# Transposing 128 keys' probabilities where the 16 meta keys are wanted, in the attention of a hybrid streaming encoder

## The chip, the cores and the metric

The kernel runs on one core of a Trainium2 chip. The metric is the device time of one launch in microseconds (us); three runs of a kernel give a median. The core has five engines with a queue of instructions each: TensorE (PE, with its weight loads shown apart as PEld), VectorE (DVE), ScalarE (ACT), GpSimd (POOL) and SyncE (SP), which here issues the DMA transfers.

## The reference, cut to what matters

One layer of a trunk over 2048 frames, with 16 learned "meta" tokens put in front (2064 positions). A combined projection feeds two mixers, an RWKV-7 recurrence and a forgetting attention with 8 heads of width 64; their outputs go through one output projection and a ConvFFN. The change lies in the attention:

```python
q = _rmsnorm(_heads(q, FX_HEADS), q_g).astype(f32) * (HEAD_DIM ** -0.5)
k = _rmsnorm(_heads(k, FX_HEADS), k_g).astype(f32)
c = jnp.cumsum(logf, axis=1)
...
    s = jnp.einsum('bhqd,bhkd->bhqk', q_i, k) + c_i[..., None] - c[:, :, None, :]
    s = jnp.where(kpos[None, :] <= pos_i[:, None], s, -jnp.inf)
    p = jax.nn.softmax(s, axis=-1)
    return jnp.einsum('bhqk,bhkd->bhqd', p, v)
```

## The kernel before, in words

**Attention.** Queries are cut into one block of the 16 meta tokens (called i = -1) and 16 blocks of 128 frames. Keys are cut in the same way: key block 0 holds the 16 meta keys, the others 128 keys each. `softmax` multiplies queries and keys in pieces of up to 512 keys into PSUM tiles `s` (two matmuls, L952 and L954, of which the second adds the low part `kl` of the keys), adds the decay row `cb` and keeps a running minimum on VectorE (L945), and takes the exponential of the whole row on ScalarE (L971) into `P`, 128 queries x all keys seen.

**Values.** `value` takes two query blocks at a time. For every key block it transposes the probabilities on TensorE into a PSUM tile `pt` (L1002: the piece of `P` is the stationary operand, an identity matrix the moving one), makes a high and a low part of the result (`ph` by a cast on ScalarE, L1017; `pl` by a subtraction on VectorE, L1018) and multiplies both with the values `vs` into the tile `o` (L1022). Key block 0 is treated apart: its transpose yields 16 rows, which go into rows 0 to 15 (high) and 32 to 47 (low) of a tile `meta` (L1011, L1012), and one matmul (L1013) adds them to `o`. There are 8 heads x 16 blocks = 128 of these 16-key transposes for blocks of 128 queries, and 8 for the block of 16 queries.

**Heads.** `load_head` brings a head's keys and queries in pieces (`raw`, L892), casts them on ScalarE (L893, L896) and subtracts on GpSimd (`kl` L894, `kq` L897); it also loads the decay row, repeated over 128 partitions (`cb`, L885, 1032 KB). `attention` is built twice: "at" (query blocks up to 7, two heads' buffers) and "at2" (query blocks 8 to 15, in which the tiles of a head, `kq`, `kl`, `cb` and `vs`, have one buffer, so that the next head's loads wait for the last score of the head before). The heads of at2 are numbered 1 to 8 below.

**What stands around it.** While the attention runs, matmuls of the projection phase (L203 to L205) and then of the output projection and the FFN (L1096) are mixed in between as filler; their weights come in pieces of 512 KB (`ww_raw`, L78), are split on ScalarE and VectorE (`ww_hi` L81, `ww_lo` L82). `xh` is the normed input of the FFN.

**What sets the order.** Nothing in the source fixes how attention and filler alternate on an engine. The whole program is built with `schedule_with_timeline_sim=True`: when the program is built, a scheduler places every instruction on a simulated timeline, and each engine's queue gets the instructions in that order. Queues run strictly in that order.

Of the kernel before, what the change touches and what calls it, by code (L numbers as in the profile page):

```python
# [855 lines left out]
def attention(K, ctx, name, phases, bufs, banks):  # L856


    nc = K.nc
# [115 lines left out]
    def keys(j):  # L975
        return (0, 16) if j == 0 else (16 + 128 * (j - 1), 128)

    def value(hd, qt, soft):

        vs, qa = hd[4], hd[6]  # L980
        nqs = [16 if i < 0 else 128 for i in qt]
        Ps, inv = zip(*soft)
        q0 = 0 if qt[0] < 0 else 16 + 128 * qt[0]
        N = sum(nqs)
        per = 2 if N <= 256 else 1
        shape = [128, per, 512 // per]
        o = ps([128, 512], "o", no)[:, :N]
        nt = qt[-1] + 2
        j = 0
        while j < nt:  # L990
            js = [j] if j == 0 else list(range(j, min(j + per, nt)))
            pt = ps(shape, "pt", npt)
            kn = keys(j)[1]
            if j:
                ph, pl = sp(shape, "ph", nph, F32R), sp(shape, "pl", nph, F32R)
            cols = []
            for x, jj in enumerate(js):
                k0, kn = keys(jj)
                c0 = 0
                for P, i, nq in zip(Ps, qt, nqs):  # L1000
                    if jj <= i + 1:
                        nc.tensor.transpose(pt[:kn, x, c0 : c0 + nq], P[:nq, k0 : k0 + kn], K.ident[:nq, :nq])  # L1002
                    c0 += nq
                cols.append(sum(nq for i, nq in zip(qt, nqs) if jj > i + 1))
            if len(set(cols)) == 1:
                views = [(slice(0, len(js)), cols[0])]
            else:
                views = [(slice(x, x + 1), c) for x, c in enumerate(cols)]
            if j == 0:
                c, p0 = cols[0], meta  # L1010
                nc.scalar.copy(p0[:kn, c:N], pt[:kn, 0, c:N])  # L1011
                nc.vector.tensor_sub(p0[32 : 32 + kn, c:N], pt[:kn, 0, c:N], p0[:kn, c:N].bitcast(F32))  # L1012
                nc.tensor.matmul(o[:, c:N], vs[:, 0], p0[:, c:N], start=True, stop=False)  # L1013
                j = 1
                continue
            for xs, c in views:
                nc.scalar.copy(ph[:kn, xs, c:N], pt[:kn, xs, c:N])  # L1017
                nc.vector.tensor_sub(pl[:kn, xs, c:N], pt[:kn, xs, c:N], ph[:kn, xs, c:N].bitcast(F32))  # L1018
            for x, jj in enumerate(js):
                c = cols[x]  # L1020
                for y, pp in enumerate((ph, pl)):
                    nc.tensor.matmul(o[:, c:N], vs[:kn, jj], pp[:kn, x, c:N], start=False, stop=jj == nt - 1 and y == 1)  # L1022
            j += len(js)
        o2 = sp([64, NQ], "o2", min(nhead, 2))[:, :N]
        nc.scalar.copy(o2, o[64:128])
        nc.vector.tensor_tensor(o2, o2, o[0:64], op=ALU.add)

        rp = ps([128, 512], "s", ns)[:, :N]
        c0 = 0
        for r, nq in zip(inv, nqs):  # L1030
            e = sp([128, 128], "E", 2)[:nq]
            nc.gpsimd.tensor_scalar(e, r.to_broadcast([nq, 128]), 1.0, 0.0, op0=ALU.mult, op1=ALU.add)
            nc.tensor.transpose(rp[:, c0 : c0 + nq], e, K.ident[:nq, :nq])
            c0 += nq
        rb = sp([64, NQ], "rb", min(nhead, 2))[:, :N]
        nc.scalar.copy(rb, rp[:64])
        og = hd[5][:, q0 - qa : q0 - qa + N]
        nc.gpsimd.tensor_tensor(og, og, rb, op=ALU.mult)
        nc.vector.tensor_tensor(og, o2, og, op=ALU.mult)

    def finish(hd, h, qt, soft, last):
        value(hd, qt, soft)
        if last:
            p_, hh = divmod(h, 2)
            og, qa = hd[5:]
            nc.sync.dma_start(K.yd[4 + p_, 64 * hh : 64 * hh + 64, qa : qa + og.shape[1]], og)
# [274 lines left out]
```

## Time and profile before

| | |
|---|---|
| median of 3 runs | 3427.64 us (3419.93 to 3429.69) |
| profiled execution | 3421.68 us, its span 3419.8 us |
| PE busy | 3321.0 us, 97% of the span |
| PEld, DVE, ACT, POOL busy | 2941.8, 2301.7, 1653.1, 1165.1 us |
| TensorE clock over the span | 0.987 of full speed |

The profile is of one execution. [...] The attention stands between 1218 and 2340 us of the span.

### The profile page before, as it was taken

The page shows a single profiled execution, that of the slowest core. Times are in us where ns is not written, and L with a number is a line of the kernel's source. Part 1 is how long each engine was busy: PE and PEld are TensorE (multiplying, and loading weights), DVE is VectorE, ACT ScalarE, POOL GpSimd, SP SyncE. Part 2 cuts the span into 40 slices and gives each one's busy share as a digit, 9 for nine tenths or more (in the row PEclk, how much of TensorE's full clock was granted, in tenths as well). Part 3 has the DMA queues.
Part 4 walks back from the last instruction along what each step waited for, and adds up shares of the span by engine and source line. Part 5 has one row for each costly group of instructions (what it writes and reads, how often), then busy time and mean ns, then how long its engine had stood idle before and what let it go on. Part 6 is the DMA issues. An engine that isn't in the chain of part 4 may idle for free.

```text
span 3419.8 us, 62536 instructions
## 1 busy us (share of the span) xinstructions
PE 3321.0 (97%) x23259; PEld 2941.8 (86%) x23259; DVE 2301.7 (67%) x4849; ACT 1653.1 (48%) x3450; POOL 1165.1 (34%) x2055
## 2 busy tenths in 40 slices
PE   7999999999999999999999999999999999999999
PEld 7889888988988988999999998888887888878887
DVE  5655566566556657888878886777665666646666
ACT  5543444554244467765666665654333333333332
POOL 4441113344111167755444454422114211132121
PEclk9999999999999999999999999999999999999999
DMA  4556333355634255333333343223324323232222
GB/s 114 119 123 161 105 95 99 102 124 130 156 88 105 84 173 160 112 103 109 94 93 94 93 137 117 86 82 129 104 89 159 97 90 97 93 116 94 93 93 92
DMA packets 352888, 376.57 MB, mean 110 GB/s; under 512 B 169112, under 2 KB 281992, under 8 KB 351560
## 3 DMA queue, kind: packets, MB, share of 16 engines
q1 hardware_dynamic: 352392, 372.52, 38.2%
q8 instruction: 183, 3.00, 0.4%
q14 instruction: 121, 0.99, 0.1%
q0 software_dynamic: 192, 0.07, 0.0%
HBM read 302.22 MB, written 70.27 MB: 109 GB/s over the span
## 4 chain that ended last, share of the span: by engine, by line
PE 51%; DVE 2%; DMA 2%; POOL 2%; issue 2%; ACT 2%; SPq 0%; POOLq 0%; ACTq 0%; DVEq 0%
PE pp L1096 30%; PE pr L1096 12%; PE o L1022 3%; PE pt L1002 3%; DMA raw<-d_qk 2%; PE s L952 1%; PE s L954 1%; DVE ww_lo L82 1%; POOL xl L1158 0%; POOL kl L894 0%; DVE P L945 0%; DVE pl L1018 0%; ACT P L971 0%; DMA cb<-d_cd 0%; ACT ph L1017 0%
## 5 line engine op out<-in xcount | busy, mean ns | idle before, releaser
L82 DVE TENSOR_TENSOR ww_lo<-ww_raw,ww_hi 128x1024 fp32r<-128x1024 f32 (+1 forms) x304 | 375.4, 1244 | 248.7 <-PE pp L1096 128.9
L81 ACT CAST ww_hi<-ww_raw 128x1024 fp32r<-128x1024 f32 (+1 forms) x304 | 307.6, 1025 | 387.9 <-PE pp L1096 140.0
L1096 PE MATMUL pp<-xh,ww_hi 128*128 128x512 f32 (+2 forms) x1952 | 432.3, 353 | 11.4 <-ACT xh L1157 6.0
L1096 PE MATMUL pp<-xh,ww_lo 128*128 128x512 f32 (+2 forms) x1952 | 429.1, 351 | 0.0
L1096 PE MATMUL pp<-xl,ww_hi 128*128 128x512 f32 (+2 forms) x1952 | 428.4, 350 | 0.3 <-POOL xl L1158 0.3
L1096 PEld LDWEIGHTS pp<-xh,ww_hi 128*128 128x128 f32 x1952 | 324.8, 190 | 66.5 <-ACT xh L1157 11.1
L1096 PEld LDWEIGHTS pp<-xl,ww_hi 128*128 128x128 f32 x1952 | 326.2, 189 | 52.8 <-POOL xl L1158 1.0
L1096 PEld LDWEIGHTS pp<-xh,ww_lo 128*128 128x128 f32 x1952 | 325.3, 189 | 47.4
L1179 POOL TENSOR_SCALAR c<-c,pc 128x1 f32<-128x1 f32 x220 | 84.7, 385 | 611.2 <-ACT c L1176 609.8
L1018 DVE TENSOR_TENSOR pl<-pt,ph 128x512 fp32r<-128x512 f32 (+2 forms) x352 | 196.1, 562 | 51.7 <-ACT ph L1017 50.1
L1191 POOL TENSOR_TENSOR zl<-cv,zh 128x512 fp32r<-128x512 f32 (+1 forms) x110 | 119.8, 1089 | 312.7 <-ACT zh L1190 302.3
L945 DVE CUSTOM_DVE_ANT_0 P<-cb,s 16x16 f32<-16x16 f32 (+8 forms) x360 | 182.7, 519 | 53.6 <-PE s L954 29.1
L1017 ACT CAST ph<-pt 128x512 fp32r<-128x512 f32 (+2 forms) x352 | 167.8, 486 | 103.4 <-PE pt L1002 72.9
L1204 DVE TENSOR_TENSOR acc<-acc,pr 128x512 f32<-128x512 f32 x240 | 164.5, 688 | 73.5 <-PE pr L1096 69.1
L1002 PE MATMUL pt<-cst,P 128*128 128x128 f32 (+2 forms) x1224 | 202.6, 277 | 2.6 <-ACT P L971 1.5
L1173 ACT ACTIVATE cv<-pp,pc 128x510 f32<-128x510 f32 (+1 forms) x220 | 151.9, 691 | 84.3 <-PE pp L1096 82.9
L89 POOL TENSOR_TENSOR wi<-sq,kx 128x320 fp32r<-128x320 f32 (+2 forms) x48 | 48.2, 1003 | 389.9 <-ACT kx L88 290.1
L203 PE MATMUL pj<-xah,w_hi 128*128 128x384 f32 x480 | 165.8, 346 | 1.6 <-ACT xah L194 1.6
L1177 DVE SCALAR_TENSOR_TENSOR cv<-pp,pc,cv 128x511 f32<-128x511 f32 (+1 forms) x220 | 140.7, 639 | 36.0 <-ACT c L1176 35.9
L205 PE MATMUL pj<-xah,w_lo 128*128 128x384 f32 x480 | 164.4, 342 | 0.4 <-DVE w_lo L82 0.4
L204 PE MATMUL pj<-xal,w_hi 128*128 128x384 f32 x480 | 163.6, 341 | 0.0
L1022 PE MATMUL o<-ph,vs 128*128 128x256 f32 x576 | 158.1, 284 | 5.5 <-ACT ph L1017 5.2
(393 smaller groups left out, 8668.8 us busy)
## 6 DMA issues: line engine op xcount, KB each, us to landing
ww_raw<-in_fin_dram SPq DMA_DIRECT2D x176, 512.0 KB, 3.6
ww_raw<-in_fout_dram SPq DMA_DIRECT2D x88, 512.0 KB, 3.7
w_raw<-in_wt_dram SPq DMA_DIRECT2D x60, 512.0 KB, 3.8
xv<-d_var SPq DMA_DIRECT2D x32, 384.0 KB, 6.0
ww_raw<-in_wo_dram SPq DMA_DIRECT2D x24, 512.0 KB, 3.6
raw<-d_qk SPq DMA_DIRECT2D x112, 88.0 KB, 2.7
cb<-d_cd SPq DMA_DIRECT2D x8, 1032.0 KB, 6.6
out_dram<-acc SPq DMA_DIRECT2D x32, 256.0 KB, 2.8
```

The source lines that it names most:

```text
L81: nc.scalar.copy(hi, raw)
L82: nc.vector.tensor_sub(lo, raw, hi.bitcast(F32))
L203: nc.tensor.matmul(p, wh[:, c, :M], xh[:, c, :n], start=c == 0, stop=False)
L204: nc.tensor.matmul(p, wh[:, c, :M], xl[:, c, :n], start=False, stop=False)
L205: nc.tensor.matmul(p, wl[:, c, :M], xh[:, c, :n], start=False, stop=c == KC - 1)
L945: nc.vector.tensor_tensor_reduce(dst, c, src, 1.0, 3e38, op0=ALU.add, op1=ALU.min, accum_out=mx[:nq, np_ : np_ + 1])
L1002: nc.tensor.transpose(pt[:kn, x, c0 : c0 + nq], P[:nq, k0 : k0 + kn], K.ident[:nq, :nq])
L1017: nc.scalar.copy(ph[:kn, xs, c:N], pt[:kn, xs, c:N])
L1018: nc.vector.tensor_sub(pl[:kn, xs, c:N], pt[:kn, xs, c:N], ph[:kn, xs, c:N].bitcast(F32))
L1022: nc.tensor.matmul(o[:, c:N], vs[:kn, jj], pp[:kn, x, c:N], start=False, stop=jj == nt - 1 and y == 1)
L1096: self.K.nc.tensor.matmul(p, w, x, start=i == 0, stop=i == len(mms) - 1)
L1204: nc.vector.tensor_tensor(a, a, p, op=ALU.add)
```

## The change

For blocks of 128 queries the transpose of key block 0 now takes the first 128 columns of `P` (`kt`), the 16 meta keys and the first 112 frame keys, and writes 128 rows of `pt`. The cast and the subtraction behind it still read 16 rows. The block of 16 queries keeps its 16 keys. The 2 lines that are added shift the line numbers behind them: L1002 becomes L1004, L1022 becomes L1024, L1096 becomes L1098.

```diff
                     if jj <= i + 1:
-                        nc.tensor.transpose(pt[:kn, x, c0 : c0 + nq], P[:nq, k0 : k0 + kn], K.ident[:nq, :nq])
+
+                        kt = 128 if i >= 0 else kn
+                        nc.tensor.transpose(pt[:kt, x, c0 : c0 + nq], P[:nq, k0 : k0 + kt], K.ident[:nq, :nq])
                     c0 += nq
```

The instructions are the same ones in number and, but for these 128, in shape. Their order is not: from about 1255 us of the span, some ten of these transposes into the attention, to about 2400 us the scheduler mixes attention and filler in another way on all five queues; before and after that stretch the queues are the same. A row below names the output tile, the inputs and the output's shape; the number at a tile's end tells its uses apart.

**TensorE, the change of head 6 to head 7 of at2** (`kq_22265` is head 7's; `pp` rows are filler). Before:

```order
L1096 MATMUL pp_29316<-xl_29098,ww_hi_29312 128x512 x5
L1096 MATMUL pp_29316<-xh_29097,ww_lo_29313 128x512 x7
L1022 MATMUL o_22151<-ph_22224,vs_21620 128x256
L1096 MATMUL pp_29316<-xh_29097,ww_lo_29313 128x512
L1096 MATMUL pp_29351<-xh_29097,ww_hi_29347 128x512 x4
L1022 MATMUL o_22151<-pl_22225,vs_21620 128x256
L1022 MATMUL o_22151<-ph_22224,vs_21620 128x256
L1022 MATMUL o_22151<-pl_22225,vs_21620 128x256
L1022 MATMUL o_22151<-ph_22237,vs_21620 128x256
L952 MATMUL s_22352<-kq_22265 128x400
```

In the changed kernel, at the same place:

```order
L1004 MATMUL pt_22425<-cst_72,P_22122 128x128
L1015 MATMUL o_22392<-meta_18159,vs_21620 128x256
L1024 MATMUL o_22392<-ph_22400,vs_21620 128x256
L1024 MATMUL o_22392<-pl_22401,vs_21620 128x256
L1024 MATMUL o_22392<-ph_22400,vs_21620 128x256
L1024 MATMUL o_22392<-pl_22401,vs_21620 128x256
L1024 MATMUL o_22392<-ph_22413,vs_21620 128x256
L952 MATMUL s_22352<-kq_22265 128x400
```

The 43 filler matmuls of 512 columns that stood between the last score of head 6 and the first score of head 7 have moved ahead of that last score; in their place stand the first products of the next pair of blocks (`o_22392`), which stood behind it before.

**ScalarE, the change of head 2 to head 3 of at2** (`ph_19417` belongs to head 2's last product, `kq_19445` to head 3's loads). Before:

```order
L1017 CAST ph_19417<-pt_19416 128x256
L893 CAST kq_19445<-raw_19458 128x336
L893 CAST kq_19445<-raw_19463 128x176
L896 CAST kq_19445<-raw_19463 128x176
L1017 CAST ph_19417<-pt_19416 128x128
L1190 CAST zh_26731<-cv_26836 128x258
```

In the changed kernel:

```order
L1019 CAST ph_19417<-pt_19416 128x256
L1019 CAST ph_19417<-pt_19416 128x128
L893 CAST kq_19445<-raw_19458 128x336
L893 CAST kq_19445<-raw_19463 128x176
L896 CAST kq_19445<-raw_19463 128x176
L1013 CAST meta_18159<-pt_19573 16x256
```

The last piece of `ph_19417` has moved from behind the three casts of freshly loaded pieces to ahead of them.

## Rows read from the trace of the kernel before

**Rows 1.** The page's head: span, instructions, busy time and share of each engine.

```profile
span 3419.8 us, 62536 instructions
PE 3321.0 (97%) x23259; PEld 2941.8 (86%) x23259; DVE 2301.7 (67%) x4849; ACT 1653.1 (48%) x3450; POOL 1165.1 (34%) x2055
```

**Rows 2.** Busy time by stretch: window, length, PE, PEld, DVE, ACT, POOL, granted clock, DMA.

```profile
1255.00:2400.00 1145.00, 1114.80 (x7854) 1036.03 (x7853) 901.71 (x2483) 714.25 (x1564) 564.90 (x1123) 0.99 0.37 111
...
1753.25:1756.60 3.35, 3.35 (x17) 3.35 (x16) 2.48 (x6) 1.78 (x5) 1.71 (x3) 0.50 0.41 107
1756.70:1800.00 43.30, 43.30 (x348) 42.78 (x347) 34.64 (x107) 28.95 (x66) 23.66 (x53) 1.00 0.33 94
...
2099.00:2132.00 33.00, 28.72 (x171) 24.21 (x171) 22.31 (x60) 20.49 (x43) 16.19 (x25) 1.00 0.29 82
```

**Rows 3.** Groups of L1002 by shape: busy us, mean ns, idle time before.

```profile
L1002 PE MATMUL pt<-cst,P 128*128 128x128 f32 x1088 | 175.8, 277 | 1.0 <-DVE meta L1012 1.0
L1002 PE MATMUL pt<-cst,P 128*16 128x128 f32 x128 | 30.2, 279 | 0.4 <-ACT P L971 0.2
...
L1002 PEld LDWEIGHTS pt<-cst,P 128*128 128x128 f32 x1088 | 128.1, 142 | 3.6 <-DVE meta L1012 1.6
...
L1002 PEld LDWEIGHTS pt<-cst,P 128*16 128x16 f32 x128 | 10.7, 89 | 1.9 <-ACT P L971 0.9 <-DVE pl L1018 0.2
```

**Rows 4.** Timeline of PE: start, length, line and shape, count of merged matmuls.

```profile
1908.17 0.60 PE L1002 MATMUL pt<-cst,P 128*128 128x128 f32 x4
...
1917.23 0.75 PE L1096 MATMUL pp<-xh,ww_lo 128*128 128x256 f32 x5
1917.81 0.28 PE L1022 MATMUL o<-ph,vs 128*128 128x256 f32 x1
...
1918.40 0.38 PE L1002 MATMUL pt<-cst,P 128*16 128x128 f32 x2
...
2088.06 2.03 PE L1096 MATMUL pp<-xh,ww_lo 128*128 128x512 f32 x8
2089.93 0.39 PE L1096 MATMUL pp<-xh,ww_hi 128*128 128x512 f32 x1
```

**Rows 5.** Scores (L952) at each change of head in at2, heads 2 to 8: first and last start.

```profile
L952 PE MATMUL s<-kq x2: 346/348/350, 1653.7 to 1665.9; 128*128 128x400 f32 x2
L952 PE MATMUL s<-kq x2: 427/554/682, 1738.6 to 1755.8; 128*128 128x400 f32 x2
L952 PE MATMUL s<-kq x2: 341/344/348, 1824.6 to 1836.5; 128*128 128x400 f32 x2
L952 PE MATMUL s<-kq x2: 340/396/451, 1906.9 to 1919.8; 128*128 128x400 f32 x2
L952 PE MATMUL s<-kq x2: 344/345/346, 1994.2 to 2007.8; 128*128 128x400 f32 x2
L952 PE MATMUL s<-kq x2: 341/382/424, 2084.7 to 2098.7; 128*128 128x400 f32 x2
L952 PE MATMUL s<-kq x2: 342/386/430, 2183.9 to 2196.9; 128*128 128x400 f32 x2
```

**Rows 6.** Timelines of POOL at the changes to heads 3, 4, 5 and 7.

```profile
1753.25 0.56 POOL L897 TENSOR_TENSOR kq<-raw,kq 64x176 fp32r<-64x176 f32 x1
...
1835.17 0.56 POOL L897 TENSOR_TENSOR kq<-raw,kq 64x176 fp32r<-64x176 f32 x1
...
1919.24 0.55 POOL L897 TENSOR_TENSOR kq<-raw,kq 64x176 fp32r<-64x176 f32 x1
...
2094.01 0.88 POOL L964 TENSOR_TENSOR cm<-cb,cst 128x128 f32<-128x128 f32 x2 [3.80 <-DMA cb<-d_cd]
...
2098.10 0.56 POOL L897 TENSOR_TENSOR kq<-raw,kq 64x176 fp32r<-64x176 f32 x1
```

**Rows 7.** Timelines of ACT and PE at the change to head 3; idle time before in brackets.

```profile
1750.82 0.80 ACT L893 CAST kq<-raw 128x336 fp32r<-128x336 f32 x2 [5.15 <-DMA raw<-d_qk]
...
1752.08 0.33 PE L1022 MATMUL o<-ph,vs 128*128 128x128 f32 x1 [3.58 <-ACT ph L1017]
```

## The prediction

> **What bounds the kernel now.** The page's head comes first: TensorE is busy for 97% of the span, no other engine for more than 67% [rows 1]. So the time is TensorE's work plus its gaps, and a change can act in two ways: it makes TensorE's work longer or shorter, or it moves gaps. The table of stretches shows the room for the second. The change touches the queues from 1255 to 2400 us; there TensorE is idle for 1145.0 - 1114.8 = 30.2 us [rows 2]. Next, the groups of L1002 by shape and TensorE's timeline price the transposes [rows 3, 4]. Last, the timelines at the places where a head of at2 gives way to the next show what decides whether TensorE waits there [rows 5 to 7]. A difference of 0.3%, 10.3 us, is about what a measurement of this kernel can tell from none.
>
> **The wider transposes.** 128 transposes take 128 columns of P as stationary operand where they took 16. The matmul streams the same 128 columns of the identity: 279 ns in the narrow form and 277 in the wide [rows 3]. What matters is what one costs in a row of them. Four wide ones take 0.60 us, so each after the first adds (0.60 - 0.28) / 3 = 0.11 us; two narrow ones take 0.38 us, so the second adds 0.38 - 0.28 = 0.10 us [rows 3, 4]. Both forms step alike. The weight load does grow, from 89 to 142 ns, 53 ns [rows 3]. It runs beside the matmul before it, and is seen only where the load itself was held back by a wait. All waits ahead of the 128 narrow loads come to 1.9 us [rows 3]. The bounds are 0 (every load hidden) and 128 x 53 ns = 6.8 us (none hidden). I take 0.5 us, some ten exposed loads, near the lower bound, since 1.9 us of waiting is the sum of few waits.
>
> [...]
>
> ScalarE's cast and VectorE's subtraction read 16 rows as before, and the wide form reads only what one exponential wrote for the whole row, so no new wait comes with it.
>
> **The changed order, at the changes of head.** In at2 a head's tiles have one buffer. Between the last score of a head and the first score of the next lies a chain: the last score frees the buffers, casts (L893) and subtractions (L894) of waiting pieces run, further pieces and the 1032 KB of `cb` are loaded, cast, and subtracted, and the first score waits for `kq` (L897). TensorE must fill that time with other rows of its queue. From the last score's start to the end of that `kq` the chain took 1753.81 - 1738.6 = 15.2 us for head 3, 1835.73 - 1824.6 = 11.1 for head 4, 1919.79 - 1906.9 = 12.9 for head 5 and 2098.66 - 2084.7 = 14.0 for head 7 [rows 5, 6]. In the last the wait for `cb` is plain, and the first score follows at 2098.7 [rows 5, 6].
>
> TensorE's work in between I count from the two orders, with a step of (2089.93 - 2088.06) / 8 = 0.233 us for a matmul of 512 columns, (1917.81 - 1917.23) / 5 = 0.12 for 256, and 0.11 for a transpose [rows 4]. For head 7, before: 43 x 0.233 + 17 x 0.11 + 15 x 0.12 + 0.36 for two score matmuls = 14.0 us, as long as the interval itself, no gap. After: 31 transposes, 24 products of 256 columns, two of 128 (0.06 each) and the two score matmuls, 3.4 + 2.9 + 0.1 + 0.4 = 6.8 us, and no filler at all. If the chain stays, TensorE stands for 14.0 - 6.8 = 7.2 us. Counted alike for heads 2 to 8, the work is 12.2, 11.6, 11.9, 11.7, 12.4, 14.0 and 12.9 us before and 13.6, 12.1, 10.0, 10.8, 15.2, 6.8 and 13.6 after. The intervals of before are 12.2, 17.2, 11.9, 12.9, 13.6, 14.0 and 13.0 us [rows 5], so before lost 0 + 5.6 + 0 + 1.2 + 1.2 + 0 + 0.1 = 8.1 us there. After, with the same chains, heads 2, 6 and 8 have more work than their interval and lose nothing; heads 3, 4, 5 and 7 lose 15.2 - 12.1 = 3.1, 11.1 - 10.0 = 1.1, 12.9 - 10.8 = 2.1 and 7.2, in all 13.5. That is **+5.4 us**. With the shortest chain seen, 11.1, everywhere, after would lose 0 + 1.1 + 0.3 + 4.3 = 5.7 us, or -2.4; I take the chains as they were, since the order of loads ahead of `cb` changes little.
>
> The gap of head 3 is not simply won, though the order removes its visible cause. A cast of `ph` stood behind three casts of pieces not yet landed; ScalarE waited 5.15 us for them and TensorE 3.58 us for `ph` [rows 7]. Now the cast stands ahead of them. But the pieces land no earlier, and what is late next is the first score of head 3; hence the 3.1 us above.
>
> **Two smaller terms.** [...] A gap of 7 us at head 7 should bring another: **+1.2**. Against that, the first products of the next pair (`o_22392`) ran from 2099 to 2132 us in a stretch with 33.0 - 28.7 = 4.3 us of idle [rows 2]; they now stand inside the wait: **-4.3**.
>
> **Sum.** 0.5 + 5.4 + 1.2 - 4.3 = +2.8 us on the profiled execution's 3421.7: 3424.5. That execution lies 6.0 us below the median of the runs, 3427.6; on the median the forecast is 3430.4, about 3430. The rest of the idle time, 30.2 - 4.3 - some 5 at the changes of head = 21 us, is dealt out anew by the new order; I see no reason for more or less of it.
>
> **The rivals.** (a) *Slower: the chains at the changes of head grow.* With chains of c us at all of them, after loses (4c - 39.7) at heads 3, 4, 5, 7 and 2(c - 13.6) at heads 2 and 8; with -8.1, +0.5, -4.3 and three more spells of half clock (3.6) that is 6c - 75.2. It passes 10.3 us from c = 14.3 on, and at head 3's 15.2 it is +16.0, 3443.6 us. For it: head 3 and head 7 had 15.2 and 14.0. Against: heads 4 and 5 had 11.1 and 12.9, and less filler in a wait also means fewer weight loads in the DMA queues. Chance 0.22. (b) *Faster: the new order fills gaps.* Of the 21 us elsewhere some 13 would have to go, beside the +2.8, to leave 3417. For it: the gaps are many, and such a one as at head 3 is undone in the order. Against: gaps of the same kind arise anew. Chance 0.11. (c) *The loads are not hidden:* 6.8 for 0.5, or 3436.7 us, still within 0.3%; slower only if waits add to it. Chance 0.04, half of it beyond. (d) *The narrow form has a hidden price*, so that the wide one is faster by itself: 2 ns of mean length x 128 = 0.3 us is all that the rows allow, and 80 ns each would be needed to be seen; chance 0.02. [...]
>
> **Chances and range.** The forecast, within 0.3%, has 0.61 and half of (c) adds 0.02: 0.63. Slower by more: 0.22 + 0.02 = 0.24. Faster by more: 0.11 + 0.02 = 0.13. The range goes from 3420, where half of the idle time elsewhere has gone (-10), to 3442, just short of (a)'s full price; about 0.08 is left out on either side.
>
> **What would show it.** L1004's 128 weight loads at about 142 ns and a step of 0.11 us; the changes of head as intervals between L952 of two heads, with about 14 us at head 7 and a TensorE gap of some 7 us in it, and half clock behind; the 3.58 us wait for `ph` gone and the wait at the first score of head 3; less idle between 2099 and 2132 us. I would be wrong if `kq` of head 7 came within 9 us of the last score, or if large gaps arose where I have not counted.

## The result and the profile after

The changed kernel took 3441.4 us, the median of 7 executions (3437.4 to 3446.7), the kernel before 3427.5 beside it. The ratio is 1.0051, with a 95% interval of 1.0033 to 1.0069: slower, by 14 us where +2.8 were forecast. In a later comparison the same program measured 1.0076 (after_again, below).

The page's head of the changed kernel, which answers to [rows 1]:

```profile
span 3440.9 us, 62529 instructions
PE 3324.6 (97%) x23259; PEld 2948.4 (86%) x23259; DVE 2314.6 (67%) x4849; ACT 1655.8 (48%) x3450; POOL 1167.4 (34%) x2055
```

The span grew by 21.1 us and TensorE's busy time by 3.6: TensorE has as much work as before and waits longer. Busy time by stretch (columns as in [rows 2]) tells where:

```profile
1255.00:2400.00 1145.00, 1099.49 (x7746) 1027.02 (x7747) 892.88 (x2461) 708.01 (x1550) 554.87 (x1113) 0.98 0.36 106
...
1250.00:1420.00 170.00, 147.41 (x1019) 134.22 (x1019) 122.73 (x375) 112.62 (x311) 111.75 (x184) 0.91 0.48 137
1420.00:1575.00 155.00, 152.48 (x1243) 150.64 (x1242) 133.90 (x404) 103.16 (x245) 91.77 (x207) 1.00 0.36 106
1575.00:2415.00 840.00, 819.60 (x5589) 758.98 (x5588) 652.15 (x1709) 500.80 (x1010) 365.86 (x732) 0.99 0.35 104
```

The same for the kernel before:

```profile
1250.00:1420.00 170.00, 158.70 (x1187) 146.69 (x1186) 128.64 (x418) 126.80 (x347) 128.78 (x217) 0.97 0.54 156
1420.00:1575.00 155.00, 153.24 (x1257) 151.31 (x1256) 136.52 (x405) 98.74 (x234) 84.68 (x192) 1.00 0.35 104
1575.00:2415.00 840.00, 822.86 (x5514) 754.91 (x5513) 647.71 (x1682) 498.59 (x1001) 356.33 (x727) 1.00 0.35 104
```

Idle time is length less PE: 45.5 us from 1255 to 2400, where [rows 2] has 30.2. Of it 22.6 lie in the first 170 us, in the part "at", with a granted clock of 0.91 over that stretch; the kernel before had 11.3 us and 0.97 there. From 1575 us on it is 20.4 against 17.1. What TensorE waited for most from 1250 to 1420 us in the changed kernel (total, times, longest; in the kernel before the longest of any wait there was 2.3 us):

```profile
PE o L1024 <- DVE pl L1020: 5.9, 4, 5.1
PE o L1015 <- DVE meta L1014: 5.4, 4, 1.7
PE o L1024 <- ACT ph L1019: 2.8, 2, 2.5
PE s L952 <- ACT rb L1038: 2.0, 2, 1.5
```

One wait of 5.1 us stands out. Here it is on TensorE's timeline, then what VectorE and GpSimd did meanwhile:

```profile
1264.20 0.22 PE L957 MATMUL s<-cmr,idr 128*128 128x128 f32 x1
1269.52 0.58 PE L1024 MATMUL o<-pl,vs 128*128 128x256 f32 x1 [5.10 <-DVE pl L1020]
```

```profile
1262.63 0.41 DVE L1014 TENSOR_TENSOR meta<-pt,meta 16x256 fp32r<-16x256 f32 x1
1263.07 5.79 DVE L1041 TENSOR_TENSOR og<-o,og 64x272 f32<-64x272 f32 x1
1268.79 0.67 DVE L1020 TENSOR_TENSOR pl<-pt,ph 128x512 fp32r<-128x512 f32 x1
```

```profile
1262.70 0.55 POOL L1034 TENSOR_SCALAR E<-nm 16x128 f32<-16x128 f32 x2
1263.23 4.66 POOL L1119 TENSOR_TENSOR xl<-acc,xh 128x1028 fp32r<-128x1028 f32 x2
1267.85 0.71 POOL L1040 TENSOR_TENSOR og<-og,rb 64x256 f32<-64x256 f32 x1
```

The trace counts the 5.79 us as the length of VectorE's product `og`, with no wait ahead of it. GpSimd runs five instructions back to back from 1262.70 to 1268.56 us. The product begins just behind the first of them (the two `E` take 0.29 us each) and ends only behind the last, after 5.79 us. That GpSimd's work is the cause is shown below by a_solo: an instruction of the same length that reads one operand, put in the place of all 64 products, takes 0.43 us at most. `pl` stands behind it in VectorE's queue, and TensorE waits for `pl`. In the kernel before, the same product and the same GpSimd rows met like this (VectorE, then GpSimd):

```profile
1263.82 0.43 DVE L1039 TENSOR_TENSOR og<-o,og 64x272 f32<-64x272 f32 x1
```

```profile
1263.94 0.73 POOL L1032 TENSOR_SCALAR E<-nm 16x128 f32<-16x128 f32 x2
1264.65 4.75 POOL L1117 TENSOR_TENSOR xl<-acc,xh 128x1028 fp32r<-128x1028 f32 x2
```

There the product began 0.12 us ahead of GpSimd's run and took 0.43 us; after, it began 0.37 us behind. Half a microsecond decides over five.

TensorE had stood for 1.5 us of this wait when its granted clock fell to 0.50, for 13.65 us:

```profile
1265.90:1279.55 13.65, 10.03 (x45) 8.97 (x46) 8.84 (x29) 6.79 (x23) 7.36 (x11) 0.50 0.37 118
```

### The profile page after: what moved, and what is told of

The parts are those of the page before. It is cut to its first block, busy times and chain, and to the rows that moved or that the text cites. A ratio compares the mean times of both kernels' runs of the same rounds, so it can differ in the third digit from the quotient of the medians.

```text
span 3440.9 us, 62529 instructions
## 1 busy us (share of the span) xinstructions
PE 3324.6 (97%) x23259; PEld 2948.4 (86%) x23259; DVE 2314.6 (67%) x4849; ACT 1655.8 (48%) x3450; POOL 1167.4 (34%) x2055
## 4 chain that ended last, share of the span: by engine, by line
PE 79%; DMA 7%; DVE 6%; issue 2%; POOL 2%; ACT 2%; SPq 1%; POOLq 0%; ACTq 0%; DVEq 0%
PE pp L1098 32%; PE pr L1098 12%; PE pj L203 5%; PE pj L205 5%; PE pj L204 5%; PE o L1024 3%; PE pt L1004 3%; DMA raw<-d_qk 2%; PE pa L737 2%; DMA xv<-d_var 2%; PE s L952 2%; PE s L954 1%; PE pb L774 1%; PE ch L802 1%; PE pb L785 1%
## 5 line engine op out<-in xcount | busy, mean ns | idle before, releaser
L1098 PE MATMUL pp<-xh,ww_hi 128*128 128x512 f32 (+2 forms) x1952 | 430.9, 353 | 9.9 <-ACT xh L1159 4.7
L1098 PE MATMUL pp<-xh,ww_lo 128*128 128x512 f32 (+2 forms) x1952 | 428.1, 351 | 0.0
L1098 PE MATMUL pp<-xl,ww_hi 128*128 128x512 f32 (+2 forms) x1952 | 427.1, 350 | 0.0
L1098 PEld LDWEIGHTS pp<-xh,ww_hi 128*128 128x128 f32 x1952 | 325.2, 190 | 63.9 <-ACT xh L1159 9.1
L1098 PEld LDWEIGHTS pp<-xl,ww_hi 128*128 128x128 f32 x1952 | 326.9, 189 | 52.0
L1098 PEld LDWEIGHTS pp<-xh,ww_lo 128*128 128x128 f32 x1952 | 325.0, 189 | 46.4
L1004 PE MATMUL pt<-cst,P 128*128 128x128 f32 (+1 forms) x1224 | 203.0, 278 | 3.8 <-ACT P L971 3.7
L1024 PE MATMUL o<-ph,vs 128*128 128x256 f32 x576 | 160.3, 288 | 7.2 <-ACT ph L1019 7.2
L1024 PE MATMUL o<-pl,vs 128*128 128x256 f32 x576 | 158.1, 293 | 8.0 <-DVE pl L1020 6.6
```

The source lines that it names most:

```text
L1004: nc.tensor.transpose(pt[:kt, x, c0 : c0 + nq], P[:nq, k0 : k0 + kt], K.ident[:nq, :nq])
L1098: self.K.nc.tensor.matmul(p, w, x, start=i == 0, stop=i == len(mms) - 1)
```

## The experiments

The scheduler orders the program by a simulated timeline, so nearly any edit deals the order anew. Two kinds of kernels get around that. In the first, operands of single instructions are replaced *after* the order is set: every engine's queue and all waits stay. In the second, a smaller part of the change gives an order that is a piece of the one and a piece of the other. This table has all 15 runs; "idle" is the window's length less PE's busy time in the profiled execution (the windows of the fences above), "clock" the granted clock. The windows are fixed in time, and the executions reach 1250 us some microseconds apart, so a microsecond or two of idle time between rows is not to be read. The profiled executions of i04, kt112 and kt96 took 3435.0, 3430.3 and 3428.9 us, some 9 to 10 us less than the medians of these kernels, so their idle columns show less than the medians lost.

| kernel | ratio to before (95%) | idle 1250-1420, clock | idle 1420-1575 | idle 1575-2415, clock |
|---|---|---|---|---|
| before | 1 | 11.3, 0.97 | 1.8 | 17.1, 1.00 |
| b_order_wide | 1.0000 (0.9989-1.0011) | 11.2, 0.98 | 1.1 | 18.9, 1.00 |
| b_short_xl | 1.0006 (0.9992-1.0021) | 11.5, 0.97 | 1.7 | 19.6, 1.00 |
| b_one_in | 0.9980 (0.9967-0.9994) | 11.8, 0.97 | 1.5 | 17.0, 1.00 |
| b_solo | 0.9999 (0.9988-1.0010) | 10.9, 0.97 | 0.7 | 16.7, 1.00 |
| b_stall | 1.0015 (1.0004-1.0026) | 15.2, 0.93 | 1.1 | 17.7, 0.99 |
| after | 1.0051 (1.0033-1.0069) | 22.6, 0.91 | 2.5 | 20.4, 0.99 |
| after_again | 1.0076 (1.0058-1.0095) | 24.7, 0.92 | 2.6 | 22.0, 0.99 |
| a_order_narrow | 1.0050 (1.0033-1.0067) | 21.7, 0.93 | 2.5 | 22.4, 0.99 |
| a_short_xl | 1.0072 (1.0054-1.0090) | 19.3, 0.92 | 2.5 | 21.4, 0.98 |
| a_one_in | 1.0066 (1.0048-1.0083) | 21.2, 0.90 | 4.0 | 18.9, 0.99 |
| a_solo | 1.0041 (1.0025-1.0058) | 14.3, 0.95 | 1.9 | 22.8, 0.99 |
| i04 | 1.0058 (1.0035-1.0080) | 18.5, 0.95 | 0.6 | 17.8, 0.99 |
| kt112 | 1.0039 (1.0023-1.0055) | 18.7, 0.94 | 0.8 | 17.7, 1.00 |
| kt96 | 1.0047 (1.0028-1.0065) | 11.2, 0.96 | 3.9 | 19.7, 0.99 |
| a_psum | 1.0045 (1.0029-1.0062) | 15.6, 0.94 | 0.8 | 22.9, 0.99 |
| b_psum | 1.0052 (1.0035-1.0069) | 15.9, 0.93 | 1.2 | 26.7, 0.99 |

**Width or order.** Two kernels swap the width and keep the order. The 128 transposes are noted as they are emitted, and rewritten once the scheduler has finished (from b_order_wide; a_order_narrow does the same to the changed kernel, with 16 for 128):

```diff
-                        nc.tensor.transpose(pt[:kn, x, c0 : c0 + nq], P[:nq, k0 : k0 + kn], K.ident[:nq, :nq])
+                        t = nc.tensor.transpose(pt[:kn, x, c0 : c0 + nq], P[:nq, k0 : k0 + kn], K.ident[:nq, :nq])
+                        if kn == 16 and i >= 0:
+                            META.add(t.ins.name)
...
+                    tile_size=(128, 32 if cols == 16 else 128), tile_position=i.tile_position, perf_mode=i.perf_mode, ldweights=i.ldweights,
...
+                    ins=[i.ins[0], view(P, [list(P.ap[0]), [1, cols]])], outs=[view(o, [[o.ap[0][0], cols], list(o.ap[1])])],
...
+    reshape_meta(nc, 128)
     r = run_bass_kernel_spmd(nc, [arrays], core_ids=[0])
```

> The instruction order of the kernel before, every engine's, with the 128 transposes of the meta keys 128 keys wide. Theory (the order that the scheduler dealt anew costs the time, not the width): ratio 1.000, 3424 to 3432 us, with 1255 to 1400 as in the kernel before. Rival (the wide weight loads cost it): 128 loads at up to 0.053 us each more, at most 6.8 us, so up to 1.002; and if width has some other price, all of 1.005 (3441 us).

> The instruction order of the changed kernel, with the 128 transposes put back to 16 keys. Theory (order): as slow as the changed kernel, ratio 1.004 to 1.006, 3437 to 3446 us, with the 5.8 us product of og near 1263 us still there. Rival (width): back to the kernel before, 1.000, or 1.003 to 1.004 if the loads carry up to 6.8 us of it.

Measured: 1.0000 and 1.0050. The wide transposes in the old order cost nothing; the narrow ones in the new order cost all of it, and the 5.8 us product is there (at 1257.87 us, 5.82). The groups of the old order with wide transposes show that the loads did grow, as in the changed kernel:

```profile
L1002 PEld LDWEIGHTS pt<-cst,P 128*128 128x128 f32 x1216 | 143.0, 142 | 4.8 <-DVE meta L1014 2.1 <-ACT P L971 0.5 <-DVE pl L1020 0.3
...
L1002 PE MATMUL pt<-cst,P 128*128 128x128 f32 x1216 | 200.9, 276 | 1.8 <-DVE meta L1014 1.5 <-ACT P L971 0.2
```

So the loss is that of the order alone.

**Which part of the order.** Three partial widenings give hybrid orders:

```diff
-                        kt = 128 if i >= 0 else kn
+                        kt = 128 if 0 <= i < 4 else kn
```

```diff
-                        kt = 128 if i >= 0 else kn
+                        kt = 112 if kn == 16 and i >= 0 else kn
```

(kt96 has 96 for 112.)

> Transposes 128 keys wide in query tiles 0 to 3 alone (64 of the 128 are widened). The order that comes of it is a hybrid: ScalarE, VectorE and GpSimd go as in the changed kernel from 1222 to 1400 us, an order of their own stands from 1400 to some 1490, and from 1572 us on it is the order of the kernel before. Theory (the loss comes from the order of 1250 to 1400, where the changed kernel fell 16 to 20 us behind): ratio 1.004 to 1.006, 3438 to 3447 us. Rival (the order of the later eight heads' part costs it): 1.000, 3423 to 3430 us.

> Transposes 112 keys wide. The order goes as in the changed kernel from 1222 to 1335 us, has a piece of its own to some 1490, and is that of the kernel before from there on. Theory: what the changed kernel had lost by 1330 us, 15 us of its 20, is lost here too: ratio 1.003 to 1.005, 3436 to 3443 us. Rival (later part): 1.000.

> Transposes 96 keys wide. The order is that of the kernel before up to 1345 us (but for two neighbours exchanged on GpSimd and three on VectorE), has a piece of its own from there to 1727 us, and is that of the changed kernel from 1727 on. Theory (only 1250 to 1400 costs): ratio 0.999 to 1.002, 3422 to 3432 us, with no og product over 2 us near 1263. Rival (the order of the later eight heads' part costs it): 1.004 or more.

Measured: 1.0058, 1.0039 and 1.0047. In i04 and kt112 the part of the new order from 1222 to 1335 us, with its rejoining piece up to 1570 or 1490, is enough for a loss of 0.4 to 0.6%: 7 us more idle time there than before, and from 1575 us on, in the old order again, 17.8 and 17.7 us, near the 17.1 of before. But kt96 failed for my theory. It has the old order in the first stretch (11.2 us idle, as before) and is as slow by its median. The first stretch suffices, and is not the only place where a new order loses.

The order of the changed kernel parts from the old one at 1222 us on VectorE, 1238 on GpSimd and 1255 on TensorE; that of i04 and kt112 follows it, on every engine, to 1397 and 1332 us. Even so the 5.8 us product is not in their traces. In i04 it began 0.14 us behind the first `E` and took 0.50 us; the two `E` took 0.79 us together, 0.55 in the changed kernel, so by these lengths it was let in ahead of the second (VectorE, then GpSimd):

```profile
1262.50 0.50 DVE L1041 TENSOR_TENSOR og<-o,og 64x272 f32<-64x272 f32 x1
```

```profile
1262.36 0.79 POOL L1034 TENSOR_SCALAR E<-nm 16x128 f32<-16x128 f32 x2
1263.13 4.74 POOL L1119 TENSOR_TENSOR xl<-acc,xh 128x1028 fp32r<-128x1028 f32 x2
```

In kt112 it began 0.23 us behind (0.43 us long); in the traces of the changed kernel and a_order_narrow, where it was held, 0.32 to 0.37. So one order can have this wait in one execution and not in another, and the 7 us of idle time in these two traces come from other waits. The 12 executions of kt112 lie from 3429.9 to 3431.8 us (four) and from 3438.1 to 3455.4 (eight); only one of the four was traced, so whether this product divides them is not shown.

**One stall taken away.** In the changed kernel, after the order was set, GpSimd's two `xl` instructions are cut from 1028 columns to 16, and the matmuls that read those parts of `xl` read `xh`. b_short_xl does the same to the kernel before.

```diff
+                L[k] = bass_rust.InstTensorTensor(
+                    name=i.name, engine=i.engine, debug=i.debug, op=i.op, acc=i.acc, ins=[view(a) for a in i.ins], outs=[view(a) for a in i.outs],
...
+    shorten_xl(nc, 16)
     r = run_bass_kernel_spmd(nc, [arrays], core_ids=[0])
```

> The changed kernel, its order kept, with GpSimd's two subtractions xl of 128x1028 (1263.2 to 1267.9 us) cut to 16 columns each; the products that read these parts of xl read xh in their place, so the low parts of four chunks are left out. Theory (the og product of VectorE stands behind these two subtractions, TensorE waits for VectorE, and the clock falls after it): og takes 0.4 us, the 6.8 us of waiting at 1263 to 1270 goes, and with it the 13.65 us at half clock, worth half of that: 10 to 14 us less than the changed kernel, 3427 to 3432 us, ratio 1.000 to 1.001. Rival (the stall is hidden, the rest of the order loses the time): 3438 us or more, ratio 1.003 or more.

> The same cut of the two subtractions in the kernel before, whose og product ran before them. Theory (only the collision costs, not GpSimd's 4.75 us as such): ratio 0.999 to 1.001. Rival (GpSimd's time there is on the path in both orders): 5 to 10 us less, ratio 0.997 to 0.9985.

Measured: 1.0072 and 1.0006. The product fell to 0.52 us, as said, though not for certain by the shorter `xl`: it began 0.12 us behind the first `E`, where the product of i04 (0.14 us behind) took 0.50 us with `xl` at full length. And yet no time was won at the end: the theory failed in its number, and the ratio is what the rival forecast (1.003 or more). Follow the `og` products, in their order, through both traces. This one starts at 1267.22 us in a_short_xl, 4.2 later than after's 1263.07; the next at 1275.39 for 1278.60, 3.2 earlier, so 7.4 us were won; fourteen further on at 1409.85 for 1409.97; one at 1573.65 for 1571.11, 2.5 later again, so 1.6 of the 7.4 are left. At the end of the span it is 12.0 behind (3452.9 for 3440.9), with the clock from 1575 us on at 0.98 for 0.99. Part of the way back is the same wait elsewhere: the products at 1322.72, 1334.38 and 1354.59 us took 2.28, 2.40 and 2.67 us for 0.57, 1.95 and 1.44. The last of these, on VectorE and beside it on GpSimd:

```profile
1354.59 2.67 DVE L1041 TENSOR_TENSOR og<-o,og 64x256 f32<-64x256 f32 x1
```

```profile
1353.78 0.46 POOL L964 TENSOR_TENSOR cm<-cb,cst 128x128 f32<-128x128 f32 x1
1354.20 0.30 POOL L1034 TENSOR_SCALAR E<-nm 128x128 f32<-128x128 f32 x1
1354.46 1.32 POOL L894 TENSOR_TENSOR kl<-raw,kq 128x528 fp32r<-128x528 f32 x1
1355.74 1.23 POOL L1119 TENSOR_TENSOR xl<-cv,xh 128x256 fp32r<-128x256 f32 x2
```

Shifted by some microseconds, other collisions take the place of the one removed.

**All of them taken away.** First try: the product becomes a copy of `og` onto itself, one operand in place of two.

```diff
+                L[k] = bass_rust.InstTensorCopy(
+                    name=i.name, engine=i.engine, debug=i.debug, ins=[i.ins[1]], outs=list(i.outs),
```

> The changed kernel, its order kept on every engine; VectorE's og product is a copy of og onto itself in its place, so it reads one operand from SBUF, not two (the factor o2 is left out). Ten such products of the changed kernel took over 1.0 us between 1255 and 1540, 20 us in all against some 5 if each took its usual 0.42 to 0.55. Theory (VectorE's product waiting for GpSimd makes most of the loss of 1250 to 1400): no such instruction over 1 us and the time back at 3424 to 3431 us, ratio 0.999 to 1.002. Rival (the order's other waits, for scores, ph and meta, make it, and whichever wait goes, the next one and the clock take its place): 3435 us or more, ratio 1.003 or more.

> The same replacement in the kernel before. It has four such products over 1.1 us between 1300 and 1530 us, some 2.9 us too long in all. Theory: 0 to 3 us less, ratio 0.999 to 1.000, so that the two orders differ by less than before. Rival (the copy gains in both orders alike): both 3 us or more below their originals.

Measured: 1.0066 and 0.9980 (0.9967 to 0.9994). In the kernel before the copy won 5.9 us, more than the 0 to 3 expected. In the changed kernel the experiment did not do what it was for, since the copy waits for GpSimd as well, whose five instructions stand from 1273.81 to 1279.68 us:

```profile
1274.19 5.65 DVE L1041 COPY og<-og 64x272 f32<-64x272 f32 x1
```

Its undisturbed length, 0.28 us for 256 columns, is two thirds of the product's, so the copy is no fair stand-in either. This pair settles nothing on the size. The second try takes an instruction that reads one operand and takes as long as the product, a sum over a single element (`og`'s factor is left out):

```diff
+                a = bass_rust.PhysicalAccessPattern(ap=[list(x) for x in a.ap] + [[0, reps]], offset=a.offset, dtype=a.dtype, memref=a.memref,
...
+                L[k] = bass_rust.InstTensorReduce(
+                    name=i.name, engine=i.engine, debug=i.debug, op=ALU.add, axis=AX.X, ins=[a], outs=list(i.outs),
...
+    reduce_in_place_of_product(nc, 0, 1)
```

> The changed kernel, its order kept on every engine; VectorE's og product is replaced by a sum over a single element, og <- o2, which reads one operand from SBUF at the ordinary rate (og's factor is left out). Theory (waits of this instruction for GpSimd make most of the loss of 1250 to 1400): none of them over 1.0 us, TensorE's idle time to 1420 us down from 22.6 by 7 or more, ratio 0.999 to 1.002, 3424 to 3431 us. Rival (another wait or the clock takes the place of each that goes): no such instruction over 1.0 us, and still 3436 us or more, ratio 1.003 or more.

> The same replacement in the kernel before, as the control: four of these instructions go from 1.1 to 1.3 us to some 0.45. Theory and rival alike: 0.998 to 1.000.

> The changed kernel once more, on the same chip as the three others, as the measure for them and for how far two profiled executions of one program differ from 1250 us on: ratio 1.0033 to 1.0069; idle time of TensorE to 1420 us 20 to 24 us, its spells at half clock up to 14 us apart from those of the first.

Now the instruction runs beside the same GpSimd work at its own length, here and in all 64 places, 0.43 us at most (VectorE, then GpSimd, of a_solo):

```profile
1266.49 0.43 DVE L1041 TENSOR_REDUCE og<-o 64x272 f32<-64x272 f32 x1
1266.84 0.67 DVE L1020 TENSOR_TENSOR pl<-pt,ph 128x512 fp32r<-128x512 f32 x1
```

```profile
1266.37 0.55 POOL L1034 TENSOR_SCALAR E<-nm 16x128 f32<-16x128 f32 x2
1266.89 4.73 POOL L1119 TENSOR_TENSOR xl<-acc,xh 128x1028 fp32r<-128x1028 f32 x2
```

Measured: a_solo 3437.7 us (1.0041), after_again 3452.5 on the same chip (1.0076), b_solo 0.9999. Idle time to 1420 us fell from 24.7 (22.6 in the first trace) to 14.3, and the clock there rose to 0.95. The medians say that the collisions cost 14.9 us of the 27.3 on that chip. Against the first measurement of the changed kernel the gain is only 3.7 us (3441.4 to 3437.7). The traces lie between: at this product a_solo is 3.4 us behind the first trace of the changed kernel (1266.49 for 1263.07), at the one at 1560.37 for 1571.11 it is 10.7 ahead, so 14.1 us were won in "at"; at the end of the span 6.2 are left (3434.7 for 3440.9). after_again goes through the same stretch 4.2 behind at the start and 4.0 at the end, so two executions of one program agree there. From the attention's first transpose to the end of the span, which leaves out what executions differ by ahead of it, the kernel before took 2200.3 us, the changed one 2221.5, 2225.1 (after_again) and 2222.2 (a_order_narrow), and a_solo 2212.3: 9 to 13 us won of 21 to 25. How far a single trace can stray is seen in b_solo, 6.7 us under the kernel before by this measure and level with it by its median. The time is what the rival forecast (1.003 or more), the idle time what the theory did (down by 7 or more): the collisions are a part of the loss, 4 to 15 us by the medians, and 12.5 us stay without them.

**The stall put into the order before.** The same reduction, 20 elements long, in place of the single product at 1263.8 us:

```diff
+    reduce_in_place_of_product(nc, 3, 20)
```

> The kernel before, its order kept; one single og product, the one that starts at 1263.8 us and takes 0.43, is replaced by a sum over 20 repeats of o2 (og's factor is left out there), which takes some 5.8 us and waits for nobody: the stall that the changed kernel has at this place, put into the other order. Theory (a stall of VectorE at this place costs for good): TensorE waits 4 to 5 us longer there, and a spell at half clock follows: 6 to 12 us, ratio 1.002 to 1.0035, 3432 to 3438 us. Rival (what is lost there is taken up later): 0.999 to 1.001.

Measured: 1.0015 (1.0004 to 1.0026), 5.1 us. VectorE's stall and TensorE's wait behind it:

```profile
1264.87 5.81 DVE L1039 TENSOR_REDUCE og<-o 64x272 f32<-64x5440 f32 x1
```

```profile
1271.09 0.59 PE L952 MATMUL s<-kq 128*128 128x272 f32 x1 [4.80 <-DVE mx L945]
```

Between this instruction's start (1.05 us later than before's) and the end of the span (3429.2 for 3419.8) b_stall lost 8.4 us; idle time there grew by 3.9 us and the granted clock over 1250 to 1420 us fell from 0.97 to 0.93. So the wait costs for good, less by the medians than the 6 to 12 us expected; the interval, 1.4 to 8.9 us, leaves its size open.

**A product that never collides, in a new order.** The sum `o2` goes back into PSUM:

```diff
-        nc.vector.tensor_tensor(o2, o2, o[0:64], op=ALU.add)
+        nc.vector.tensor_tensor(o[0:64], o2, o[0:64], op=ALU.add)
...
-        nc.vector.tensor_tensor(og, o2, og, op=ALU.mult)
+        nc.vector.tensor_tensor(og, o[0:64], og, op=ALU.mult)
```

> The changed kernel with the sum o2 put back into o's PSUM buffer, so that VectorE's og product reads one operand from SBUF in place of two; the order is dealt anew by it. Theory (a VectorE product with both operands in SBUF waits for GpSimd's running subtraction, one with an operand in PSUM does not): no og product over 1.0 us in the whole trace (before and after have 4 and 6 such between 1255 and 1450 us). The time hangs on the new order: if the collision makes most of the loss, 3425 to 3432 us; if any new order here can lose as much by its other waits, 3436 or more.

> The kernel before with the sum o2 put back into o's PSUM buffer, so that the og product reads one operand from SBUF; transposes 16 keys wide; the order is dealt anew. Four other orders have measured 1.0039 to 1.0058. Theory (nearly any other order loses 10 to 20 us against this one): 1.003 to 1.007, though no og product is over 1.0 us. Rival (taking the collisions out of the kernel before gives a faster one): 0.997 to 1.000.

Measured: 1.0045 and 1.0052. No `og` product over 1.0 us is left in either trace, and both are as slow as the changed kernel: their orders have 22.9 and 26.7 us of idle time from 1575 us on, where before had 17.1. No kernel here beats the kernel before with all of the work done.

## Why the prediction was wrong

The forecast, no change by more than 0.3%, was wrong. That the median of 3441.4 us lies just inside its range is luck: the upper end of 3442 came from the price of rival (a), growing chains, which is not what cost the time, and the 3452.5 of after_again lies outside. By its steps:

- **The wider transposes (+0.5).** Right. The loads grew from 89 to 142 ns, the matmul stayed at 276 to 278, and in the old order the kernel with wide transposes measures 1.0000 (0.9989 to 1.0011, so 3.8 us at most). The 6.8 us of rival (c) do not appear: the loads are hidden. Rival (d) falls too: the kernel before, narrow, is no slower than b_order_wide. The two steps that the prediction compared, 0.11 and 0.10 us, could not show it, since each stands between two transposes of one form.
- **The changes of head in at2 (+5.4).** Near in the sum, in part by luck. The stretches from the last score of a head to the first of the next, heads 2 to 8, in the changed kernel:

```profile
1671.50:1687.00 15.50, 14.08 (x118) 13.87 (x117) 9.46 (x27) 9.51 (x23) 9.91 (x20) 1.00 0.46 137
1766.30:1778.60 12.30, 12.30 (x106) 12.30 (x106) 8.67 (x24) 8.95 (x17) 6.70 (x11) 1.00 0.44 130
1849.80:1862.20 12.40, 10.85 (x87) 10.26 (x86) 7.50 (x17) 10.20 (x21) 7.68 (x14) 1.00 0.58 171
1935.10:1949.20 14.10, 11.46 (x94) 11.03 (x93) 9.09 (x22) 9.77 (x22) 9.16 (x19) 0.98 0.48 152
2023.90:2043.60 19.70, 17.20 (x133) 17.00 (x132) 13.01 (x32) 11.88 (x23) 14.52 (x17) 0.91 0.63 191
2128.10:2143.20 15.10, 10.96 (x69) 9.62 (x68) 8.41 (x21) 9.00 (x19) 10.07 (x14) 0.77 0.47 140
2227.20:2241.10 13.90, 13.90 (x74) 11.83 (x74) 8.85 (x17) 8.72 (x16) 6.24 (x10) 1.00 0.67 203
sum 103.00, PE 90.75 PEld 85.91 DVE 64.99 ACT 68.01 POOL 64.28; mean PE 12.96 PEld 12.27 DVE 9.28 ACT 9.72 POOL 9.18
```

  The sum of the same seven stretches before:

```profile
sum 96.30, PE 90.97 PEld 85.74 DVE 61.71 ACT 62.47 POOL 57.91; mean PE 13.00 PEld 12.25 DVE 8.82 ACT 8.92 POOL 8.27
```

  Idle in them: 103.00 - 90.75 = 12.3 us after and 96.30 - 90.97 = 5.3 before, +6.9 for +5.4. Head by head the count was off: 0, 3.1, 1.1, 2.1, 0, 7.2 and 0 us were forecast, 1.4, 0, 1.6, 2.6, 2.5, 4.1 and 0 measured. The wait that the prediction describes, of the first score for `kq`, stands at heads 2, 4 and 5 (1.4, 1.5 and 1.3 us). At head 7 `kq` came 13.8 us behind the last score's start, as forecast (14.0), but more work stood there than counted, some of it small matmuls that I had left out, some at half clock, and the longest wait, 2.9 us, is of such a small matmul (L103) for GpSimd's `E` (L100), which stood behind GpSimd's wait for the loads. At head 6 the stretch grew to 19.7 us and its 2.5 us are a filler matmul's wait for `ww_hi`; `kq` was ready 3 us ahead of the first score, so this is not rival (a). At head 3 the 3.58 us wait of [rows 7] is gone, and the first score, expected late, waited for nothing.
- **Half clock (+1.2) and the stretch at 2099 (-4.3).** The second is right: behind head 7, from 2143.2 to 2176 us, 0.4 us of idle time are left of the 4.3. Over all of 1575 to 2415 us idle time grew by 3.3 us, 6.9 at the changes of head and -3.6 elsewhere. Half clock came at heads 5, 6 and 7, 13.6 us in all (6.7 in the same range before), 6.8 of them at head 7: more than the one spell of 3.35 us that the prediction added. No run shows the 1.2 us that its sum takes for a spell (3.6 for three in rival (a)): that was my estimate from the spell behind head 3's gap [rows 2]. At head 7, in place of this, 19 matmuls stood in 6.80 us at a clock of 0.50, in which TensorE was busy for 3.88:

```profile
2136.30:2143.10 6.80, 3.88 (x19) 3.48 (x18) 3.01 (x6) 3.25 (x8) 3.87 (x7) 0.50 0.57 173
```

- **"The rest of the idle time [...] is dealt out anew by the new order; I see no reason for more or less of it."** This step failed. I counted TensorE's queue at seven places of at2 and left the part "at" at zero, though [rows 2] covers it too. There idle time doubled, from 11.3 to 22.6 us, with spells at half clock. The prediction had named this as a sign that it would be wrong: large gaps where none had been counted. Runs i04 and kt112 show that this part of the order alone makes the kernel slower by 0.4 to 0.6%; a_order_narrow that the width has no part in it; a_solo that VectorE's waits for GpSimd are a share of it, b_stall that one such wait costs some 5 us. Rival (b) held that gaps elsewhere might be filled; that they might as well double was given no chance.

What stays open: the 12.5 us that a_solo keeps. Idle time from 1575 us on, 22.8 us for the 17.1 of before, is part of it; the rest, with the spells at half clock, wasn't taken apart, nor were the waits by which i04, kt112 and kt96 lose. Also open is why the same program measured 1.0051 and 1.0076 in two comparisons; the intervals meet between 1.0058 and 1.0069.

## What to carry to other kernels

Where a scheduler orders the program by a model, an edit that costs nothing can still be slow by the order that it deals: here the width cost 0.0% and the order 0.5%, and all six new orders that were tried lost 0.4 to 0.8% against this one. Separate the two early: rewrite the operands after the order is set, or make the edit only where the order stays. And a count of what stands in one engine's queue misses a loss that two other engines make by holding each other up: look in the trace for instructions that take many times their usual length.

## What the runs showed of the hardware

- A VectorE product with both inputs in SBUF that began 0.37 us behind the first of five GpSimd instructions in a row took 5.79 us and ended 0.3 us behind the last of them (changed kernel; begun 0.32 us behind, 5.82 us in a_order_narrow; 5.86 us in after_again). Begun 0.14 and 0.23 us behind the first, it took 0.50 us (i04) and 0.43 (kt112).
- A copy from SBUF to SBUF, 0.28 us for 256 columns where nothing held it, took 5.65 us beside the same GpSimd work (a_one_in); a reduction with one input took 0.43 us at most (a_solo), and of the products with one input in PSUM none took over 1.0 us (a_psum, b_psum).
- In a TensorE wait of 5.1 us in the changed kernel the granted clock fell to 0.50 and stayed there for 13.65 us; in these TensorE was busy for 10.03 us and did 45 matmuls. So a wait can cost more than its own length: in the trace of b_stall 3.9 us more idle time went with 8.4 us lost.
